# Layer norm roots of two tiles at once, gates ahead of the GLU, and GLU products in time order in a decoder trunk kernel

## The chip, the cores and the metric

The kernel runs on one core of one Trainium2 chip. Times are device microseconds of a whole execution. TensorE (PE) multiplies matrices, VectorE (DVE) and GpSimd (POOL) work on tensors elementwise, ScalarE (ACT) evaluates functions out of a table that has to be loaded, and SyncE (SP) issues most of the DMAs.

## The reference, cut to what matters

One layer of a hybrid recurrent trunk for a prompt of 2048 tokens and 32 sample tokens, with a model width of 1024. The part that the change touches, in short form:

```python
r  = sigmoid(xa_c @ w_r + b_r);  gi = sigmoid(xa_c @ w_i + b_i)   # RG-LRU gates, 8 heads of 64
log_a = -8 * r * softplus(-lam); a = exp(log_a)
mult = sqrt(-expm1(2 * log_a))
hseq = linear_scan(a, mult * gi * xa_c, h0)
y_a  = gelu(gate_a) * hseq
gy   = gelu(y_s)                                  # y_s: output of the S5 recurrence
y_b  = gy * sigmoid(gy @ glu_w + glu_b)           # the GLU
mix  = concat([y_a, y_b], -1) @ out_proj
x    = layer_norm(ALPHA * x + g1 * mix, ln1_g, ln1_b)
h    = x * (1 + sc2) + sh2                        # then the MLP, with a second layer norm
```

## The kernel before, in words

All matmuls keep single precision by splitting each operand into a high and a low part (`split`: ScalarE copies the high part, another engine subtracts to get the low part); a product is then three matmuls, high by high, high by low and low by high.

The program runs in stages. First come modulation, the input projection and the S5 recurrence. Then comes the stage of this change, from about 440 to 760 us: it walks over eight blocks `pi` of 256 tokens (the last has the 32 sample tokens too), and each block goes through

- `rg_gates`: eight PSUM tiles `pg` of three matmuls each; ScalarE takes a sigmoid of each into `rr` and `gi`, and a tanh of `rr` into `th`.
- `rg_scan`: ScalarE's exponential of `rr`, its square (into `xc`), VectorE's `th`, ScalarE's square root, GpSimd's products `gi`, VectorE's scan over time (`gi`), the product `gt`, and the split of `gt` into `yah` and `yal`.
- `glu_in` and `glu_block`: loads `gy` and splits it into `gyh` and `gyl`; four PSUM tiles `glu` of twelve matmuls each; a tanh on ScalarE (a sigmoid of half the argument), a product with `gy` on VectorE, and for every two of the four tiles a split into `ybh` and `ybl`. The S5 output lies in memory by (i, c), where a token's time is 8c+i; the split reads with a stride, so that `ybh` and `ybl` are in time order.
- `rg_conv`: the depthwise convolution that prepares the gates' operand `xc`, split into `xch` and `xcl`.
- `out_block`: for the two tiles of 128 tokens, two halves of 512 columns each, 24 matmuls of 512 columns into a PSUM tile `op`, VectorE's product with the gate row `g1r`, VectorE's sum with the residual `x`, then `norm`: statistics, the reciprocal root `rs` by an integer estimate and three Newton steps on columns of 128x1 (`rstd_of`), the normalization, eight transposes through PSUM tiles `nt`, and a store.

The loop works on several blocks at once: in pass `pi` it does the GLU of block pi+1, the gates of block pi+2, the out products of block pi, then the scan of block pi+2 and the convolution of block pi+3. A scheduler then orders each engine's instructions by readiness; the written order is its guide. Two things bind it: `after_all` lists that keep ScalarE's instructions of one table together (gates and GLU use tanh and sigmoid, the scan exponentials and square root), and the buffers. Gates and GLU take turns in the PSUM tags A and B, of two buffers each (`rot(GLU_BANKS)`), the out products in D and B (`rot(OUT_BANKS)`); so B is shared by all three. `raw_tile` gives the x tiles of `out_block` three buffers of 128x1024.

Of the kernel before, what the change touches and what calls it, by code (L numbers as in the profile page):

```python
# [9 lines left out]
F32 = mybir.dt.float32  # L10
# [3 lines left out]
ALU = mybir.AluOpType  # L14
# [12 lines left out]
L = 8  # L27
# [8 lines left out]
def trunk(ctx: ExitStack, tc: tile.TileContext, *args):  # L36
# [18 lines left out]
    def ts(eng, out, in0, s1, s2=None, op0=ALU.mult, op1=ALU.add):  # L55
        if s2 is None:
            eng.tensor_scalar(out, in0, s1, None, op0)  # L57
        else:
            eng.tensor_scalar(out, in0, s1, s2, op0, op1)

    def stt(out, in0, s, in1, op0=ALU.mult, op1=ALU.add):
        return V.scalar_tensor_tensor(out, in0, s, in1, op0, op1)  # L62
# [560 lines left out]
    ts(V, ab1, vec["ln1_b"], ALPHA, None, ALU.mult)  # L623
    add(V, AB, AB, ab1.unsqueeze(2).to_broadcast([P, KD, 9]))

    def rstd_of(pool, mv, nm, np_):
        r = pool.tile([P, 1], F32, tag="rstd", name=nm, bufs=2)[:np_]
        v = pool.tile([P, 1], F32, tag="rvar", name=nm + "v", bufs=2)[:np_]
        t = pool.tile([P, 1], F32, tag="rtmp", name=nm + "t", bufs=2)[:np_]
        ts(V, v, mv[:, 1:2], EPS, None, ALU.add)  # L630
        V.tensor_scalar(t.bitcast(I32), v.bitcast(I32), 1, None, ALU.arith_shift_right)
        V.tensor_scalar(r.bitcast(I32), t.bitcast(I32), -1.0, 1597463007.0, ALU.mult, ALU.add)
        ts(V, v, v, -0.5, None, ALU.mult)
        for _ in range(3):
# [204 lines left out]
    def glu_in(pi):  # L839
        last = pi == 7  # L840
        npr = 256
        n = npr + (TS if last else 0)
        c0, ncp = pi * 32, 32
        ncc = ncp + (16 if last else 0)
        if pi:
            gy = p4.tile([P, 4, 288], F32, tag="gy", name=f"gy{pi}")
        else:
            gy = raw_tile("gy0").rearrange("p (f t) -> p f t", f=4)
        for f in range(4):
            SP.dma_start(gy[:, f, :npr].rearrange("p (i c) -> p i c", i=L),  # L850
                         Yd[f, :, :, c0:c0 + ncp].rearrange("i p c -> p i c"))
        if last:
            Q.tensor_copy(gy[:, :, npr:n], ysm)
        if pi:
            gyh = p4.tile([P, 4, 288], F32R, tag="gyh", name=f"gyh{pi}")
            gyl = p4.tile([P, 4, 288], F32R, tag="gyl", name=f"gyl{pi}")
        else:
            gyh, gyl = (wslot("gy0", x, wpb).rearrange("p (f t) -> p f t", f=4) for x in "hl")
        split(gyh[:, :, :n], gyl[:, :, :n], gy[:, :, :n], Q)
        return gy, gyh, gyl  # L860

    gy0 = glu_in(0)
# [33 lines left out]
    def glu_block(pi):  # L896
        last = pi == 7
        npr = 256
        n = npr + (TS if last else 0)
        gy, gyh, gyl = glu_in(pi) if pi else gy0  # L900
        yh = p4.tile([P, 4, 288], F32R, tag="ybh", name=f"ybh{pi}", bufs=2)
        yl = p4.tile([P, 4, 288], F32R, tag="ybl", name=f"ybl{pi}", bufs=2)
        glu_t = []
        for m in range(4):
            ms = slice(m * P, m * P + P)
            ac = gate_ps[0](f"glu{pi}_{m}")
            for k in range(4):
                wh, wl = gw[k // 2]
                kk = k % 2
                PE.matmul(ac[:, :n], wh[:, kk, ms], gyh[:, k, :n], start=(k == 0), stop=False)  # L910
                PE.matmul(ac[:, :n], wh[:, kk, ms], gyl[:, k, :n], start=False, stop=False)
                PE.matmul(ac[:, :n], wl[:, kk, ms], gyh[:, k, :n], start=False, stop=(k == 3))
            glu_t.append(act(ac[:, :n], ac[:, :n], AF.Tanh, scale=0.5, bias=hgb[:, m:m + 1]))
            stt(gy[:, m, :n], ac[:, :n], 1.0, gy[:, m, :n], ALU.add, ALU.mult)
            if m % 2:
                ms = slice(m - 1, m + 1)
                split(yh[:, ms, 0:npr].rearrange("p f (c i) -> p f c i", i=L),
                      yl[:, ms, 0:npr].rearrange("p f (c i) -> p f c i", i=L),
                      gy[:, ms, 0:npr].rearrange("p f (i c) -> p f c i", i=L), V)
                if last:  # L920
                    split(yh[:, ms, npr:n].rearrange("p f (s j) -> p f s j", j=JS),
                          yl[:, ms, npr:n].rearrange("p f (s j) -> p f s j", j=JS),
                          gy[:, ms, npr:n].rearrange("p f (j s) -> p f s j", j=JS), Q)
        if pi:
            after_all(rgs[pi]["root"], glu_t)
        if pi < 7:
            rgs["glu", pi + 1] = glu_t
        return yh, yl

    def out_block(pi, ya, yb):  # L930
        t0 = pi * 256
        tiles = ([(256, TS, True)] if pi == 7 else []) + [(0, P, False), (P, P, False)]
        for ti, (o, w, smp) in enumerate(tiles):
            xt = raw_tile(f"x4_{pi}_{ti}")
            SP.dma_start(xt[:w, :], xs if smp else xp[t0 + o:t0 + o + w, :])
# [13 lines left out]
            for half in range(2):  # L949
# [26 lines left out]
    def norm(pi, ti, xt, w, smp, t, pool):

        st = pool.tile([P, 2, 6], F32, tag="st5", name=f"st_{pi}_{ti}", bufs=2)
        mv = pool.tile([P, 2], F32, tag="mv5", name=f"mv_{pi}_{ti}", bufs=2)
        for half in range(2):  # L980
            V.bn_stats(st[:w, half, :], xt[:w, half * 512:half * 512 + 512])
        V.bn_aggr(mv[:w], st[:w])
        rs = rstd_of(pool, mv[:w], f"rs4_{pi}_{ti}", w)
        ts(V, xt[:w], xt[:w], mv[:w, 0:1], rs, ALU.subtract, ALU.mult)
# [12 lines left out]
        (S if pi == 7 else SP).dma_start(Nd[:, :, t:t + w].rearrange("k p t -> p k t"), nT[:, :, :w])
# [901 lines left out]
```

## Time and profile before

| what | value |
|---|---|
| median of three runs | 2111.79 us (2110.53 to 2115.14) |
| the profiled execution | 2115.44 us, its span 2113.7 us |
| TensorE busy | 2011.9 us, 95% of the span |
| VectorE busy | 1543.5 us, 73% |
| ScalarE busy | 1087.4 us, 51% |
| GpSimd busy | 494.0 us, 23% |
| TensorE's mean granted clock | 0.986 of full |

The span is what the profiler saw of the program; the execution's time has 1.7 us more around it. The last chain of work, followed back from the end, is 63% TensorE and 19% VectorE. The shares are means over stages that differ: the stage of this change is the part from about 440 to 760 us, and behind it stands the MLP, where TensorE works almost without a pause.

### The profile page before, as it was taken

What the parts mean: (1) busy time and instruction counts of PE and PEld (TensorE: products, weight loads), DVE (VectorE), ACT (ScalarE), POOL (GpSimd) and SP (SyncE); (2) the same over time, 40 slices, a digit from 0 to 9 for tenths busy, and PEclk for the clock granted to TensorE, in tenths of its full rate; (3) what the DMA queues carried; (4) which work ended last, traced back from release to release, by engine and by line L of the source; (5) the groups of instructions that cost most, each with busy time, mean ns of one, the idle gap of its engine ahead of it and who ended that gap; (6) DMA issues with size and microseconds to landing.
All of it is one profiled execution on the core that took longest, in us unless ns stands there. A gap on an engine that the chain in (4) does not pass through costs nothing.

```text
span 2113.7 us, 35579 instructions
## 1 busy us (share of the span) xinstructions
PE 2011.9 (95%) x13055; PEld 1904.1 (90%) x13055; DVE 1543.5 (73%) x2920; ACT 1087.4 (51%) x2077; POOL 494.0 (23%) x327
## 2 busy tenths in 40 slices
PE   7998999889999989999999899999999999999996
PEld 4897888887877879999999899999999999999996
DVE  5678897467887899989898965666747555655587
ACT  3446665445766447554646454635445344444452
POOL 2255333323433233222223300101012001010103
PEclk9999999999999999999999999999999999999998
DMA  9799765543434467968677797878678968686861
GB/s 329 177 263 274 233 197 171 141 137 80 130 94 99 134 244 265 346 248 306 239 278 264 266 323 248 305 268 288 243 260 317 315 229 282 216 270 239 265 218 54
DMA packets 363037, 489.08 MB, mean 231 GB/s; under 512 B 126939, under 2 KB 264575, under 8 KB 362863
## 3 DMA queue, kind: packets, MB, share of 16 engines
q1 hardware_dynamic: 359415, 485.52, 69.6%
q8 instruction: 103, 1.69, 0.3%
q10 hardware_dynamic: 3448, 1.29, 0.2%
q14 instruction: 71, 0.58, 0.1%
HBM read 347.73 MB, written 139.00 MB: 230 GB/s over the span
## 4 chain that ended last, share of the span: by engine, by line
PE 63%; DVE 19%; DMA 6%; issue 5%; ACT 4%; POOL 1%; SPq 1%; ACTq 0%; DVEq 0%; POOLq 0%
PE m1a L1078 19%; PE m2x L1225 13%; PE m1s L1078 8%; PE m2s L1225 6%; PE m2a L1225 3%; DVE xc L62 2%; DVE acc L44 1%; PE accg L373 1%; PE accg L374 1%; PE accg L375 1%; PE op L963 1%; PE pa L185 1%; PE op L964 1%; PE op L962 1%; DVE gi L347 1%
## 5 line engine op out<-in xcount | busy, mean ns | idle before, releaser
L44 POOL TENSOR_TENSOR y<-y,ln_g 128x512 f32<-128x512 f32 (+3 forms) x28 | 36.5, 1320 | 645.8 <-ACT y L65 544.2
L65 ACT ACTIVATE hid<-hid 128x346 f32<-128x346 f32 (+1 forms) x240 | 116.1, 489 | 71.1 <-DVE hid L62 64.3
L65 ACT ACTIVATE ht<-hid 128x692 fp32r<-128x692 f32 (+1 forms) x92 | 72.0, 783 | 127.8 <-PE m2a L1225 38.9
L44 DVE TENSOR_TENSOR lt<-hid,ht 128x692 fp32r<-128x692 f32 (+1 forms) x92 | 85.2, 927 | 40.5 <-ACT ht L65 40.5
L44 DVE TENSOR_TENSOR acc<-m2x,acc 128x346 f32<-128x346 f32 (+1 forms) x168 | 84.1, 511 | 32.0 <-PE m2x L1225 31.7
L44 DVE TENSOR_TENSOR hid<-hid,hid 128x692 f32<-128x692 f32 (+1 forms) x92 | 87.1, 947 | 23.5 <-ACT hid L65 23.3
L1225 PE MATMUL m2x<-ht,hw2s 128*128 128x348 f32 (+1 forms) x352 | 87.7, 322 | 1.8 <-DVE acc L44 1.8
L62 DVE SCALAR_TENSOR_TENSOR hid<-m1s,vecB,u 128x346 f32<-128x346 f32 (+1 forms) x94 | 53.5, 573 | 45.0 <-ACT u L65 35.4
L65 ACT ACTIVATE u<-m1a 128x346 f32<-128x346 f32 (+1 forms) x96 | 43.5, 453 | 70.4 <-PE m1a L1078 63.0
L44 DVE TENSOR_TENSOR lb<-hid,hb 128x692 fp32r<-128x692 f32 (+1 forms) x69 | 69.2, 1004 | 4.7 <-ACT hb L65 4.5
L65 ACT ACTIVATE hb<-hid 128x692 fp32r<-128x692 f32 (+1 forms) x69 | 53.8, 783 | 21.6 <-PE m2a L1225 6.9
L1225 PEld LDWEIGHTS m2x<-ht,hw2s 128*128 128x128 f32 x352 | 61.9, 189 | 2.2 <-ACT hw2s L65 2.1
L65 ACT ACT_TABLE_LOAD x40 | 51.3, 1283 | 15.9 <-DVE hgb L57 6.5
L44 DVE TENSOR_TENSOR acc<-m2s,acc 128x346 f32<-128x346 f32 (+1 forms) x120 | 55.7, 508 | 4.1 <-PE m2s L1225 4.0
L1078 PE MATMUL m1s<-h2t13h,hw1s 128*128 128x348 f32 (+1 forms) x200 | 54.1, 329 | 3.9 <-DVE x L62 3.5
L1225 PE MATMUL m2x<-lt,hw2s 128*128 128x348 f32 (+1 forms) x176 | 56.1, 321 | 0.9 <-DVE lt L44 0.9
L1225 PE MATMUL m2x<-ht,w2s 128*128 128x346 f32 (+1 forms) x216 | 55.9, 321 | 0.0
L1225 PE MATMUL m2s<-ht,hw2s 128*128 128x348 f32 (+1 forms) x208 | 53.2, 331 | 2.6 <-ACT ht L65 2.6
L44 DVE TENSOR_TENSOR u<-m1s,u 128x346 f32<-128x346 f32 (+1 forms) x48 | 24.7, 514 | 42.0 <-PE m1s L1078 27.2
L65 ACT ACTIVATE y<-y,AB,mods 128x128 f32<-128x128 f32 (+2 forms) x96 | 37.5, 472 | 34.5 <-DMA y<-Cd 34.5
L1225 PE MATMUL m2a<-hb,hw2a 128*128 128x348 f32 (+1 forms) x200 | 52.0, 327 | 3.4 <-DVE acc L44 3.4
L1078 PE MATMUL m1a<-h2b1h,hw1a 128*128 128x348 f32 (+1 forms) x208 | 55.1, 323 | 0.0
(854 smaller groups left out, 7982.0 us busy)
## 6 DMA issues: line engine op xcount, KB each, us to landing
W1d<-hw1s SPq DMA_DIRECT2D x53, 512.0 KB
W2d<-hw2s SPq DMA_DIRECT2D x53, 512.0 KB
w1s<-W1d SPq DMA_DIRECT2D x45, 512.0 KB
lw1s<-W1d SPq DMA_DIRECT2D x43, 512.0 KB
hw2s<-W2d SPq DMA_DIRECT2D x41, 512.0 KB
hw1s<-W1d SPq DMA_DIRECT2D x40, 512.0 KB
w2s<-W2d SPq DMA_DIRECT2D x40, 512.0 KB
lw2s<-W2d SPq DMA_DIRECT2D x39, 512.0 KB
```

The source lines that it names most:

```text
L44: return eng.tensor_tensor(out=out, in0=in0, in1=in1, op=op)
L62: return V.scalar_tensor_tensor(out, in0, s, in1, op0, op1)
L65: return S.activation(out, in_, f, **kw).ins
L185: PE.matmul(pa[q:q + 32, :], cT[:, k + e, :], w[:, n * 512:n * 512 + 512], start=(k == 0), stop=(k == KD - 2), tile_position=(0, q))
L347: V.tensor_tensor_scan(gi[:, f, :n], rr[:, f, :n], gi[:, f, :n], 0.0 if pi == 0 else rgs["h"][:, f:f + 1], ALU.mult, ALU.add)
L373: PE.matmul(acc[:, :nt], wh[:, k, :], hh[:, kk, :nt], start=(k == 0), stop=False)
L374: PE.matmul(acc[:, :nt], wh[:, k, :], hl[:, kk, :nt], start=False, stop=False)
L375: PE.matmul(acc[:, :nt], wl[:, k, :], hh[:, kk, :nt], start=False, stop=(k == KD - 1))
L962: PE.matmul(ac[:w, :], yh[:, kk, o:o + w], wh[:, hs], start=(k == 0), stop=False)
L963: PE.matmul(ac[:w, :], yl[:, kk, o:o + w], wh[:, hs], start=False, stop=False)
L1078: PE.matmul(ps, x[:, k, :], h[:, k, o:o + w], start=(on is None and k + i == 0), stop=(k == 3 and i == 2), skip_group_check=on is not None)
L1225: PE.matmul(ps[2 * s_ + jj], x[:, f, js], h[:, f, :], start=(fresh and n + f + e == 0), stop=(n == len(pairs) - 1 and f + e == 3), skip_gr ...
```

## The change

Four edits in one stage. (1) The norm takes both tiles of a block together: two variances stand side by side in a 128x2 tile, and one root chain serves both; a Newton step is written as two products and one fused step where it was two fused steps. The last block's three tiles still go one by one. (2) The GLU product writes into a new tile `gp` in time order, and the split reads `gp` in a row; before, the product was written over `gy` and the split read with the stride. (3) The gates of block pi+2 are written ahead of the GLU of block pi+1, and the table order now puts the GLU's tanhs behind the first sigmoid of the next gates and ahead of the exponentials, in one table. (4) The low part `gyl` of the GLU's input is subtracted on VectorE, where GpSimd did it.

```diff
-    def rstd_of(pool, mv, nm, np_):
...
-        ts(V, v, mv[:, 1:2], EPS, None, ALU.add)
+    def rstd_of(pool, var, nm, np_):
+        r, v, t = (pool.tile([P, 2], F32, tag=tag, name=nm + tag, bufs=2)[:np_, :var.shape[1]]
+                   for tag in ("rstd", "rvar", "rtmp"))
+        ts(V, v, var, EPS, None, ALU.add)
...
         for _ in range(3):
-            stt(t, r, v, r, ALU.mult, ALU.mult)
+            mul(V, t, r, r)
+            mul(V, t, t, v)
             stt(r, t, 1.5, r, ALU.add, ALU.mult)
...
-        split(gyh[:, :, :n], gyl[:, :, :n], gy[:, :, :n], Q)
+        split(gyh[:, :, :n], gyl[:, :, :n], gy[:, :, :n], V)
...
+        gp = p4.tile([P, 4, 288], F32, tag="gp", name=f"gp{pi}")
...
-            stt(gy[:, m, :n], ac[:, :n], 1.0, gy[:, m, :n], ALU.add, ALU.mult)
+
+            stt(gp[:, m, 0:npr].rearrange("p (c i) -> p i c", i=L), ac[:, 0:npr].rearrange("p (i c) -> p i c", i=L), 1.0,
+                gy[:, m, 0:npr].rearrange("p (i c) -> p i c", i=L), ALU.add, ALU.mult)
+            if last:
+                stt(gp[:, m, npr:n], ac[:, npr:n], 1.0, gy[:, m, npr:n], ALU.add, ALU.mult)
             if m % 2:
                 ms = slice(m - 1, m + 1)
-                split(yh[:, ms, 0:npr].rearrange("p f (c i) -> p f c i", i=L),
-                      yl[:, ms, 0:npr].rearrange("p f (c i) -> p f c i", i=L),
-                      gy[:, ms, 0:npr].rearrange("p f (i c) -> p f c i", i=L), V)
+                split(yh[:, ms, 0:npr], yl[:, ms, 0:npr], gp[:, ms, 0:npr], V)
...
-        if pi:
+        if 0 < pi < 7:
+
+            after_all(rgs[pi + 1]["sig"][:1], glu_t)
+        elif pi:
             after_all(rgs[pi]["root"], glu_t)
         if pi < 7:
-            rgs["glu", pi + 1] = glu_t
+            rgs["glu", pi] = glu_t
...
+        if pi < 7:
+            norm(both_, p4)
...
+    def norm(tiles, pool):
+
+        pi, ti = tiles[0][:2]
+        w = tiles[0][3]
+        mv = pool.tile([P, 2, 2], F32, tag="mv5", name=f"mv_{pi}_{ti}", bufs=2)
+        for e, (_, ti_, xt, *_) in enumerate(tiles):
+            st = pool.tile([P, 2, 6], F32, tag="st5", name=f"st_{pi}_{ti_}", bufs=2)
+            for half in range(2):
+                V.bn_stats(st[:w, half, :], xt[:w, half * 512:half * 512 + 512])
+            V.bn_aggr(mv[:w, e, :], st[:w])
+        rs = rstd_of(pool, mv[:w, 0:len(tiles), 1], f"rs4_{pi}_{ti}", w)
+        for e, tile_ in enumerate(tiles):
+            norm_out(*tile_, mv[:, e, 0:1], rs[:, e:e + 1], pool)
...
     for pi in range(8):
+        if pi < 6:
+            rg_gates(rg, pi + 2)
         if pi < 7:
             ybs[pi + 1] = glu_block(pi + 1)
-        if pi < 6:
-            rg_gates(rg, pi + 2)
```

What the scheduler makes of it is seen in each engine's order. Names carry the block (glu3_1 is the second GLU tile of block 3) and a serial number. The first place is ScalarE around the GLU of block 3. Before, its tanhs have a table load on either side, and the gates of block 4 (rr4, gi4) come behind the second load:

```order
L65 ACTIVATE th3_6512<-th3_6512 128x4x256
L65 ACTIVATE yah3_6753<-gt3_6735 128x4x256
L65 ACT_TABLE_LOAD
L65 ACTIVATE glu3_0_6791<-glu3_0_6791,hgb_5928 128x256
L65 ACTIVATE glu3_1_6806<-glu3_1_6806,hgb_5928 128x256
L65 ACTIVATE glu3_2_6823<-glu3_2_6823,hgb_5928 128x256
L65 ACTIVATE ybh3_6789<-gy3_6780 128x2x256
L65 ACTIVATE glu3_3_6838<-glu3_3_6838,hgb_5928 128x256
L65 ACT_TABLE_LOAD
L65 ACTIVATE rr4_6855<-pg4_0_0_6858,vecB_250 128x256
```

Of the change, the same tanhs on ScalarE:

```order
L65 ACTIVATE rr4_6761<-pg4_3_0_6794,vecB_250 128x256
L65 ACTIVATE th4_6763<-rr4_6761,nla_100 128x256
L65 ACTIVATE gi4_6762<-pg4_2_1_6789,vecB_250 128x256
L65 ACTIVATE gi4_6762<-pg4_3_1_6799,vecB_250 128x256
L65 ACTIVATE glu3_0_6820<-glu3_0_6820,hgb_5928 128x256
L65 ACTIVATE xch5_7076<-xc5_7075 128x4x256
L65 ACTIVATE glu3_1_6835<-glu3_1_6835,hgb_5928 128x256
L65 ACTIVATE glu3_2_6852<-glu3_2_6852,hgb_5928 128x256
L65 ACTIVATE ybh3_6817<-gp3_6819 128x2x256
L65 ACTIVATE glu3_3_6867<-glu3_3_6867,hgb_5928 128x256
L65 ACT_TABLE_LOAD
L65 ACTIVATE rr4_6761<-rr4_6761,la_99 128x256 x4
```

The tanhs moved behind the gates of block 4 with no load between, the exponentials (rr4 out of la) follow one load later, and the conversion xch5 stands among the tanhs.

The second place is VectorE around a scan. Before, in block 3, the scan (gi3) and the product gt3 have steps of a root chain (rs4_1_0) around them:

```order
L631 TENSOR_SCALAR rs4_1_0t_6620<-rs4_1_0v_6619 128x1
L347 SCALAR_TENSOR_TENSOR gi3_6511<-rr3_6510,hp2_6405,gi3_6511 128x256 x4
L632 TENSOR_SCALAR rs4_1_0_6618<-rs4_1_0t_6620 128x1
L57 TENSOR_SCALAR rs4_1_0v_6619<-rs4_1_0v_6619 128x1
L350 COPY hp3_6750<-gi3_6511 128x4
L44 TENSOR_TENSOR gt3_6735<-gt3_6735,gi3_6511 128x4x256
L62 SCALAR_TENSOR_TENSOR rs4_1_0t_6620<-rs4_1_0_6618,rs4_1_0v_6619 128x1
L44 TENSOR_TENSOR op1_1_1_6675<-op1_1_1_6675,g1r_6052 128x512
L62 SCALAR_TENSOR_TENSOR rs4_1_0_6618<-rs4_1_0t_6620,rs4_1_0_6618 128x1
```

Of the change, VectorE around the scan of block 4:

```order
L62 SCALAR_TENSOR_TENSOR th4_6763<-xc4_6740,th4_6763 128x4x256
L44 TENSOR_TENSOR gyl4_7149<-gy4_7143,gyh4_7148 128x4x256
L44 TENSOR_TENSOR op2_0_1_6913<-op2_0_1_6913,g1r_6053 128x512
L347 SCALAR_TENSOR_TENSOR gi4_6762<-rr4_6761,hp3_6731,gi4_6762 128x256 x3
L44 TENSOR_TENSOR op2_1_0_6942<-op2_1_0_6942,g1r_6053 128x512
L347 SCALAR_TENSOR_TENSOR gi4_6762<-rr4_6761,hp3_6731,gi4_6762 128x256
L62 SCALAR_TENSOR_TENSOR x4_2_0_6884<-x4_2_0_6884,op2_0_1_6913 128x512
L62 SCALAR_TENSOR_TENSOR x4_2_1_6940<-x4_2_1_6940,op2_1_0_6942 128x512
L350 COPY hp4_7066<-gi4_6762 128x4
L44 TENSOR_TENSOR gt4_7051<-gt4_7051,gi4_6762 128x4x256
L995 BN_STATS st_2_0_6997<-x4_2_0_6884 128x6
```

The new subtraction gyl4 stands ahead of the scan, and behind the scan come the residual's sums and statistics where root steps stood.

The third place is TensorE where the gates begin. Before, the gates of block 3 (pg3) follow the GLU of block 2:

```order
L910 MATMUL glu2_3_6493<-gyh2_6440,hglu1_5924 128x256
L911 MATMUL glu2_3_6493<-gyl2_6441,hglu1_5924 128x256
L912 MATMUL glu2_3_6493<-gyh2_6440,lglu1_5925 128x256
L311 MATMUL pg3_0_0_6513<-xch3_6415,wgh_4961 128x256
L312 MATMUL pg3_0_0_6513<-xcl3_6416,wgh_4961 128x256
L313 MATMUL pg3_0_0_6513<-xch3_6415,wgl_4962 128x256
```

Of the change, the gates of block 4 on TensorE:

```order
L969 MATMUL op1_1_1_6634<-hwo7_5974,ybh1_6147 128x512
L970 MATMUL op1_1_1_6634<-hwo7_5974,ybl1_6148 128x512
L971 MATMUL op1_1_1_6634<-lwo7_5975,ybh1_6147 128x512
L311 MATMUL pg4_0_0_6764<-xch4_6741,wgh_4961 128x256
L312 MATMUL pg4_0_0_6764<-xcl4_6742,wgh_4961 128x256
L313 MATMUL pg4_0_0_6764<-xch4_6741,wgl_4962 128x256
L311 MATMUL pg4_1_0_6774<-xch4_6741,wgh_4961 128x256
L312 MATMUL pg4_1_0_6774<-xcl4_6742,wgh_4961 128x256
L313 MATMUL pg4_1_0_6774<-xch4_6741,wgl_4962 128x256
L969 MATMUL op2_0_0_6886<-hwo1_5938,yah2_6399 128x512
```

The gates now begin right behind the out products of block 1, with the out products of block 2 among them.

## Rows read from the trace of the kernel before

**Rows 1.** Windows: start:end, length, busy PE, PEld, DVE, ACT, POOL; clock, DMA share, GB/s

```profile
520.00:668.00 148.00, 135.16 (x741) 114.08 (x741) 126.18 (x288) 100.43 (x151) 56.51 (x27) 0.99 0.38 101
760.00:2113.00 1353.00, 1315.83 (x8240) 1304.28 (x8238) 970.12 (x1658) 663.75 (x1249) 231.69 (x157) 0.99 0.76 263
```

**Rows 2.** Timeline of TensorE, 505.9 to 518.7 us: start, duration, engine, line, operation

```profile
506.04 0.39 PE L963 MATMUL op<-hwo,ybl 128*128 128x512 f32 x1
...
514.19 0.28 PE L910 MATMUL glu<-gyh,hglu 128*128 128x256 f32 x1
...
518.31 0.28 PE L912 MATMUL glu<-gyh,lglu 128*128 128x256 f32 x1
```

**Rows 3.** Timeline of ScalarE, the first and last of six loads before exponentials

```profile
505.17 1.28 ACT L65 ACT_TABLE_LOAD   x1
...
681.26 1.28 ACT L65 ACT_TABLE_LOAD   x1
```

**Rows 4.** TensorE's waits, 466 to 668 us: who, for whom, total us, times, longest

```profile
PE pg L311 <- DVE gy L62: 4.4, 7, 1.2
PE glu L910 <- DVE x L62: 3.9, 3, 1.7
PE nt L995 <- DVE x L59: 3.6, 4, 2.4
PE op L962 <- ACT ybh L65: 2.9, 1, 2.9
PE op L963 <- DVE ybl L44: 1.2, 2, 0.9
```

**Rows 5.** Timeline of all engines, 520.9 to 525 us; brackets: idle before, releaser

```profile
521.01 0.15 DVE L62 SCALAR_TENSOR_TENSOR rs<-rs_0t,rs 128x1 f32<-128x1 f32 x1
...
521.59 2.37 POOL L44 TENSOR_TENSOR yal<-gt,yah 128x1024 fp32r<-128x1024 f32 x1 [5.27 <-ACT yah L65]
521.74 2.23 DVE L62 SCALAR_TENSOR_TENSOR rs_0t<-rs,rs_0v 128x1 f32<-128x1 f32 x1
...
523.90 0.41 DVE L62 SCALAR_TENSOR_TENSOR gy<-glu,gy 128x256 f32<-128x256 f32 x1
...
524.36 0.38 PE L311 MATMUL pg<-xch,wgh 128*128 128x256 f32 x1 [0.80 <-DVE gy L62]
```

**Rows 6.** Groups of VectorE by shape, 466 to 760 us: busy us, mean ns | idle

```profile
L44 DVE TENSOR_TENSOR ybl<-gy,ybh 128x512 fp32r<-128x512 f32 x16 | 18.5, 1156 | 2.0 <-ACT ybh L65 1.9
L62 DVE SCALAR_TENSOR_TENSOR rs_0t<-rs,rs_0v 128x1 f32<-128x1 f32 x21 | 13.7, 653 | 0.2
...
L62 DVE SCALAR_TENSOR_TENSOR gy<-glu,gy 128x256 f32<-128x256 f32 x28 | 11.5, 416 | 1.9 <-ACT glu L65 1.9
...
L44 DVE TENSOR_TENSOR gt<-gt,gi 128x1024 f32<-128x1024 f32 x5 | 6.1, 1218 | 0.0
...
L44 DVE TENSOR_TENSOR hw1a<-rw,hw1a 128x512 fp32r<-128x512 f32 x2 | 1.4, 677 | 2.7 <-ACT hw1a L65 2.7
```

**Rows 7.** Groups of ScalarE by shape, 466 to 760 us

```profile
L65 ACT ACT_TABLE_LOAD x28 | 35.9, 1283 | 7.4 <-DVE hgb L57 6.5 <-issue 0.4
L65 ACT ACTIVATE ybh<-gy 128x512 fp32r<-128x512 f32 x16 | 18.4, 1147 | 13.6 <-DVE gy L62 13.6
...
L65 ACT ACTIVATE hw1a<-rw 128x512 fp32r<-128x512 f32 x2 | 1.3, 626 | 5.1 <-DMA rw<-in_mlp_w_dram 5.1
```

**Rows 8.** Groups of GpSimd by shape, 466 to 760 us

```profile
L44 POOL TENSOR_TENSOR gyl<-gy,gyh 128x1024 fp32r<-128x1024 f32 x6 | 16.0, 2675 | 49.4 <-ACT gyh L65 49.4
```

**Rows 9.** The chain that ended last, 538 to 548 us: start, duration, what

```profile
540.28 5.05 DMA x<-in_x_prompt_dram
```

**Rows 10.** Timeline of ScalarE, 539 to 546 us

```profile
539.83 1.06 ACT L65 ACTIVATE xch<-xc 128x1024 fp32r<-128x1024 f32 x1 [1.40 <-DVE xc L62]
```

**Rows 11.** Windows of 20 us: columns as in rows 1

```profile
560.00:580.00 20.00, 20.00 (x98) 17.06 (x98) 13.08 (x32) 15.78 (x27) 7.34 (x4) 0.93 0.57 145
760.00:780.00 20.00, 17.08 (x90) 14.95 (x88) 18.84 (x42) 9.76 (x20) 7.10 (x4) 0.90 0.88 305
```

More of the change, by code (lines that the diff above doesn't have):

```diff
@@ L624, in trunk @@
     add(V, AB, AB, ab1.unsqueeze(2).to_broadcast([P, KD, 9]))
-    def rstd_of(pool, mv, nm, np_):
-        r = pool.tile([P, 1], F32, tag="rstd", name=nm, bufs=2)[:np_]
-        v = pool.tile([P, 1], F32, tag="rvar", name=nm + "v", bufs=2)[:np_]
-        t = pool.tile([P, 1], F32, tag="rtmp", name=nm + "t", bufs=2)[:np_]
-        ts(V, v, mv[:, 1:2], EPS, None, ALU.add)
+    def rstd_of(pool, var, nm, np_):
+        r, v, t = (pool.tile([P, 2], F32, tag=tag, name=nm + tag, bufs=2)[:np_, :var.shape[1]]
+                   for tag in ("rstd", "rvar", "rtmp"))
+        ts(V, v, var, EPS, None, ALU.add)
         V.tensor_scalar(t.bitcast(I32), v.bitcast(I32), 1, None, ALU.arith_shift_right)
@@ L922, in glu_block @@
                           yl[:, ms, npr:n].rearrange("p f (s j) -> p f s j", j=JS),
-                          gy[:, ms, npr:n].rearrange("p f (j s) -> p f s j", j=JS), Q)
-        if pi:
+                          gp[:, ms, npr:n].rearrange("p f (j s) -> p f s j", j=JS), Q)
+        if 0 < pi < 7:
+            after_all(rgs[pi + 1]["sig"][:1], glu_t)
+        elif pi:
             after_all(rgs[pi]["root"], glu_t)
         if pi < 7:
-            rgs["glu", pi + 1] = glu_t
+            rgs["glu", pi] = glu_t
         return yh, yl
@@ L932, in out_block @@
         tiles = ([(256, TS, True)] if pi == 7 else []) + [(0, P, False), (P, P, False)]
+        both_ = []
         for ti, (o, w, smp) in enumerate(tiles):
@@ L966, in out_block, with norm_out @@
                 stt(xt[:w, hs], xt[:w, hs], ALPHA, ac[:w, :])
-            work = lambda *x, at=(pi, ti, xt, w, smp, t0 + o): norm(*at, *x)
+            at = [(pi, ti, xt, w, smp, t0 + o)]
             if pi == 7 and ti in DEFER:
-                deferred.append(work)
-            else:
-                work(p4)
+                deferred.append(lambda pool, at=at: norm(at, pool))
+            elif pi == 7:
+                norm(at, p4)
+            else:
+                both_ += at
+        if pi < 7:
+            norm(both_, p4)
     DEFER = (1, 2)
     deferred = []
[L976 to L984, printed above, removed]
+    def norm(tiles, pool):
[10 more added lines that the diff above has]
+            norm_out(*tile_, mv[:, e, 0:1], rs[:, e:e + 1], pool)
+    def norm_out(pi, ti, xt, w, smp, t, mean, rs, pool):
+        ts(V, xt[:w], xt[:w], mean[:w], rs, ALU.subtract, ALU.mult)
         if smp:
```

## The prediction

> **What bounds the kernel now.** The profiled execution took 2115.4 us, a span of 2113.7 and 1.7 around it; the three runs shown have their median at 2111.8, so this execution lies 3.7 us above it. I make the sum against the 2115.4 and carry the difference over to the median unchanged.
>
> The view by windows comes first [rows 1]. The changed code runs before 760 us; in the 1353 us after it nothing is edited. So the change plays out in about 290 us, and its worth is what TensorE stands still there. In the steady blocks (520 to 668 us) TensorE is busy 135.2 us of 148, VectorE 126.2, ScalarE 100.4, GpSimd 56.5: TensorE ends last, with VectorE close behind it, at 85%.
>
> How long a block has to be comes from the spacing of matmuls at full clock [rows 2]: 35 steps with 512 columns from 506.04 to 514.19, 0.233 us each; 35 with 256 from 514.19 to 518.31, 0.118 each. A block of 256 tokens has 96 of the first and 72 of the second (24 for gates, 48 for GLU), 22.4 + 8.5 = 30.9 us, and 16 transposes besides. What a block takes is the distance of the exponentials' table loads: from 505.17 to 681.26 are five blocks [rows 3], 35.2 us each. Some 4 us a block are transposes and standstill.
>
> The view of TensorE's waits names the standstill [rows 4]. Gates wait for GLU products 7 times (4.4 us), GLU matmuls for residual adds (3.9), transposes for the normalized x (3.6), out products for the high and low parts of the GLU output (2.9 and 1.2). These five rows make 16.0 us in 202: the ceiling of what the order of work can bring.
>
> Why a product is late is seen in a timeline [rows 5]. A step of the root chain on a 128x1 column takes 0.15 us at 521.01; the same kind of step takes 2.23 at 521.74, and ends at 523.97 when GpSimd's subtraction yal (521.59 plus 2.37) ends. The GLU product starts behind it, at 523.90, and the gates' matmul at 524.36. VectorE's instructions with two tensors in SBUF stand still while GpSimd runs a tensor_tensor. [...]
>
> **The change, part by part.**
>
> *Order on TensorE (gates ahead of GLU).* The gates' first buffers, of tags A and B, were last read by the GLU's products long before and by the out block's adds; the GLU then follows the gates, whose readers are ScalarE's sigmoids. No gate comes right behind a product any more: T1, the 4.4 us of gates behind products, go: −4.4. Bounds 0 (another reader is as late) and −4.4. The 3.9 us for which GLU matmuls waited for the residual adds pass to the gates, which now take those banks first. They may stay whole (0) or go whole (−3.9), because the added 12 matmuls of work ahead give VectorE time; I take half, T2 = −2.0.
>
> *Norm of two tiles at once.* Root chains of 20 small instructions a pair become one of 13: seven fewer at 0.15 us [rows 5], −1.05 us of VectorE a block. More matters that 21 steps which wrote rs_0t took 653 ns in the mean [rows 6], so each can be caught behind GpSimd. Behind the scan now stand statistics and adds out of PSUM, one SBUF input each. On the other side the first tile's transposes come later, with the second's. T3, of the 3.6 us that transposes wait: a quarter, −0.9 (bounds 0 and −3.6). The last block does its three tiles alone, with 13 instructions where there were 10: nine more at 0.15 make T6 = +1.4, in a stretch (760 to 780 us) where VectorE is busy 18.8 us of 20 [rows 11]. Bounds 0 and +1.4.
>
> *GLU products in time order.* The product now writes with a stride of eight elements (32 bytes), and the split after it reads in a row. What the split gains stands in rows: the low part took 1156 ns [rows 6], a subtraction of the same size read in a row 677 (hw1a); the high part on ScalarE 1147 against 626 [rows 7]. Two halves a block: 0.96 us less on VectorE, 1.04 on ScalarE. What the strided write costs no row shows. Lower bound: nothing, the product stays at 416 ns [rows 6]. Upper bound: the same price for each element as the strided read, (1156−677)/2 = 0.24 us for 256 columns, four times 0.96 a block. I take the upper end, since the strided read is its nearest row; then VectorE gains nothing by this edit and ScalarE its 1.04. [...] The out products' wait for these parts: the last high and low parts come 0.52 and 0.48 us sooner after their product, and gates standing between cover up to 12×0.118 = 1.4. Of 4.1 us I let the first and a single piece of cover through: T4 = −1.9 (0 to −4.1).
>
> *One table for GLU and gates.* Three table loads a block instead of four; 40 become 36 in all, at 1.28 us [rows 7] 5.1 us of ScalarE. ScalarE has some 11 us a block free (47.6 of 148 us idle, of 35.2), so alone this is worth nothing; it shortens the way from yah to the gates. I cost it at nothing beyond T1 and T2. Its cover is that slack.
>
> *Conversions ahead of the GLU.* In some blocks xch, the split of the convolution, now stands among the GLU tanhs. It waited 1.40 us for VectorE's xc and took 1.06 in a block of before [rows 10]. Queued behind it are the tanhs, behind these the products, ybh, and the out products. Three blocks at 1.40 are 4.2 us on ScalarE; a third reaches TensorE, T7 = +1.4 (0 to +4.2).
>
> *gyl on VectorE.* GpSimd loses 2675 ns a block [rows 8]; VectorE gets it at the price of gt, the same shape with two inputs, 1218 ns [rows 6]. It cancels the −1.05 of the roots. It stands right before the scan, so the scan, gt and yah wait behind it; the out products read this yah only two blocks later, but on ScalarE the next gates' table load and sigmoids are queued behind yah, and TensorE's gates wait for their banks. Cost on the path: nothing while ScalarE's 11 free microseconds cover it; without cover 1.22 a block, 7.3 for six (rival A).
>
> [...]
>
> **Sum.** −4.4 −2.0 −0.9 −1.9 −1.4 +1.4 +1.4 = −7.8 us. Execution 2115.4 to 2107.6, median 2111.8 to 2104.0 (−0.37%). No change means within 0.2% (4.2 us), about what a measurement of this kernel can tell. With each term a third off, its own range is 2100 to 2108.
>
> **Rivals.**
>
> *A, same: the loop through ScalarE and VectorE sets the pace.* Gates, GLU tanh, exponential, square, root, scan, yah and the next gates now follow each other under fixed tables, on VectorE with gyl (1.22) and a product (0.66 with the upper bound) ahead of the scan. For it: VectorE is busy 85% of the stretch, so its queue has 5.2 us of a block's 35.2 left. Against it: two of three new pieces are paid for by the roots and the low parts. Then T1 and T2 come back as a wait for another reader, and −0.9 −1.9 +1.4 +1.4 leaves 0; 2109 to 2113. Chance 0.20.
>
> *B, slower: the pair keeps two of three raw buffers.* A tile's buffer was given back after its own transposes; now both come free after the pair's. The second x of the next block can be loaded only then. Such a load took 5.05 us and ended a chain that the residual add waited for [rows 9]. The add follows 11.2 us (48×0.233) after the first tile's; it decides when the transposes end less than 5.05 us ahead of the add. In VectorE's order, products and statistics stand behind it. At 3 us in six blocks, +18: −7.8 +18 is 2122. Against it: the pair's transposes stand ahead of half a block's matmuls. Chance 0.14.
>
> *C, more.* All five waits of [rows 4] go, 16.0, and the dip of 1.4, with T6 alone, +1.4, against them: −16.0, 2096. For it: every one has VectorE's queue at its root. Against: VectorE's load stays what it is. Chance 0.12.
>
> *D: the table does not merge.* The instructions as ordered have 36 loads, so this holds only if GLU tanhs come too late and stall it; 2112, chance 0.02.
>
> My forecast has 0.52. **Chances**: faster 0.50 + 0.12, and a hundredth of D, 0.63; same 0.02 + 0.20, 0.22; slower B and a hundredth, 0.15. **Range**: from C with T5 at −2.8 and T6 at 0, −18.8, 2093, to A's 2113 with T7 at its upper end, 2.8 more, 2116; it leaves B out.
>
> **What would show it.** Right: gates (pg) no longer wait for gy or gp; GLU waits for x gone or under 2 us; 36 table loads; exponentials' loads 33.5 to 34.5 us apart; products gp near 0.66 us, low parts near 0.68, gyl near 1.22; fewer root steps over 1 us. Wrong: x adds idle behind the DMA of x (B); scan or ybh behind gyl, with gates waiting for ScalarE (A); gp over 0.9 us; or a clock below 0.97 in a further stretch of 20 us.

## The result and the profile after

The change made the kernel slower: 2124.1 us median of six runs (2122.2 to 2127.3) against 2113.3 of before (2110.5 to 2115.1), a ratio of 1.0055 with a 95% interval of 1.0042 to 1.0068, so 9 to 14 us. The forecast was 2104, and its range ended at 2116. The profiled execution took 2127.05 us, 11.6 more than before's.

The waits of TensorE in the profile after, 466 to 668 us, answer to [rows 4]:

```profile
PE pg L311 <- DVE x L62: 7.5, 3, 5.4
PE nt L1013 <- DVE x L59: 5.9, 3, 3.4
PE pg L311 <- ACT rr L65: 2.4, 3, 1.1
PE pg L311 <- DVE gp L62: 1.9, 1, 1.9
PE op L969 <- DVE gp L62: 1.0, 1, 1.0
```

The gates wait for gy no more, but for x, rr and gp, 11.8 us in place of 4.4. The 3.9 us of GLU behind x, of which half was to go, are 7.5 of gates behind x; the transposes' wait for the normalized x went from 3.6 to 5.9. The sum is 18.7 us, against 16.0 for the five rows of before.

The windows of the profile after have the columns of [rows 1]:

```profile
520.00:668.00 148.00, 131.63 (x691) 109.54 (x690) 125.27 (x248) 84.28 (x136) 39.86 (x20) 0.97 0.36 98
```

VectorE issued 248 instructions where it had issued 288 and was busy as long, 125.3 us against 126.2. The two counts aren't for equal work: the pair norm takes away seven small steps a block, some thirty in this window, and TensorE got through fewer matmuls in it (691 against 741). What held the gates up is seen at their longest wait. The timelines of VectorE and GpSimd in the profile after, 645 to 661 us:

```profile
651.50 2.39 POOL L44 TENSOR_TENSOR gi<-gi,th 128x1024 f32<-128x1024 f32 x1 [2.75 <-ACT th L65]
...
652.33 2.63 DVE L44 TENSOR_TENSOR gyl<-gy,gyh 128x1024 fp32r<-128x1024 f32 x1 [2.44 <-ACT gyh L65]
654.89 0.68 DVE L44 TENSOR_TENSOR op<-op,g1r 128x512 f32<-128x512 f32 x1
655.49 2.66 DVE L347 TENSOR_TENSOR_SCAN gi<-rr,hp,gi 128x256 f32<-128x256 f32 x4
658.08 0.66 DVE L62 SCALAR_TENSOR_TENSOR x<-x,op 128x512 f32<-128x512 f32 x1
```

and that of TensorE, 652 to 660 us:

```profile
653.02 0.40 PE L969 MATMUL op<-hwo,yah 128*128 128x512 f32 x1
658.79 0.61 PE L311 MATMUL pg<-xch,wgh 128*128 128x288 f32 x1 [5.37 <-DVE x L62]
```

VectorE waits 2.44 us for ScalarE's gyh, then gyl takes 2.63 us (1.22 was its price): GpSimd's product has been running when gyl starts, and gyl ends 1.07 us after that product, which ended at 653.89. Then come the scans, and the residual sum that gives the gates their buffer starts at 658.08. TensorE stands for 5.4 us.

### The profile page after: what moved, and what is told of

Its sections match the earlier page's. It is cut to its first block, busy times and chain, and to the rows that moved or that the text cites. A ratio compares the mean times of both kernels' runs of the same rounds, so it can differ in the third digit from the quotient of the medians.

```text
span 2125.3 us, 35513 instructions
## 1 busy us (share of the span) xinstructions
PE 2018.1 (95%) x13055; PEld 1908.6 (90%) x13055; DVE 1546.3 (73%) x2892; ACT 1074.1 (51%) x2073; POOL 484.9 (23%) x319
## 4 chain that ended last, share of the span: by engine, by line
PE 63%; DVE 19%; DMA 6%; issue 4%; ACT 4%; POOL 2%; SPq 1%; ACTq 0%; DVEq 0%; POOLq 0%
PE m1a L1096 19%; PE m2x L1243 13%; PE m1s L1096 8%; PE m2s L1243 6%; PE m2a L1243 3%; DVE xc L62 2%; DVE acc L44 1%; PE pa L185 1%; DMA xa<-Xd 1%; PE accg L373 1%; PE accg L374 1%; DVE hw2s L44 1%; PE accg L375 1%; PE op L970 1%; PE op L971 1%
## 5 line engine op out<-in xcount | busy, mean ns | idle before, releaser
L44 DVE TENSOR_TENSOR lb<-hid,hb 128x692 fp32r<-128x692 f32 (+1 forms) x69 | 63.7, 925 | 6.2 <-ACT hb L65 6.1
L969 PE MATMUL op<-hwo,yah 128*128 128x512 f32 x128 | 52.0, 407 | 3.2 <-ACT os L65 2.2
L62 DVE SCALAR_TENSOR_TENSOR E<-E,et 128x16 f32<-128x16 f32 (+3 forms) x128 | 46.1, 399 | 10.3 <-ACT et L65 10.1
```

What stands on the lines that cost most here:

```text
L44: return eng.tensor_tensor(out=out, in0=in0, in1=in1, op=op)
L969: PE.matmul(ac[:w, :], yh[:, kk, o:o + w], wh[:, hs], start=(k == 0), stop=False)
```

## The experiments

Each kernel was timed beside the kernel before; the ratio is to that, with its 95% interval. The parts are called norm (both tiles at once), gyl (on VectorE), product (GLU products in time order) and order (gates ahead, one table).

| kernel | median us | ratio | interval |
|---|---|---|---|
| the change | 2124.1 | 1.0055 | 1.0042 to 1.0068 |
| without gyl (m1) | 2125.2 | 1.0064 | 1.0050 to 1.0078 |
| without order (m2) | 2111.4 | 0.9997 | 0.9988 to 1.0006 |
| without norm (m3) | 2116.2 | 1.0016 | 1.0005 to 1.0028 |
| without product (m4) | 2118.3 | 1.0026 | 1.0016 to 1.0037 |
| order alone (o1) | 2129.9 | 1.0081 | 1.0067 to 1.0095 |
| norm alone (o2) | 2117.1 | 1.0026 | 1.0016 to 1.0035 |
| without order, last block's steps fused (o3) | 2110.9 | 0.9992 | 0.9983 to 1.0001 |
| change, out products in own buffers (o4) | 2125.6 | 1.0059 | 1.0045 to 1.0072 |
| change, two rr and gi (x1) | 2124.9 | 1.0061 | 1.0048 to 1.0074 |
| without order, one table (x2) | 2112.7 | 1.0002 | 0.9992 to 1.0013 |
| gyl and product alone (x3) | 2111.0 | 0.9999 | 0.9987 to 1.0011 |
| the same, one table (x4) | 2116.3 | 1.0019 | 1.0009 to 1.0030 |
| without gyl, two rr and gi (y1) | 2122.5 | 1.0049 | 1.0037 to 1.0061 |
| change, two rr and gi, own buffers (y2) | 2128.6 | 1.0079 | 1.0067 to 1.0091 |
| the same without gyl (y3) | 2127.1 | 1.0071 | 1.0059 to 1.0083 |
| without order, two rr and gi (y4) | 2111.7 | 0.9997 | 0.9986 to 1.0008 |
| change, less GpSimd work (h1) | 2115.2 | 1.0014 | 1.0002 to 1.0026 |
| without order, less GpSimd work (h2) | 2112.2 | 1.0009 | 0.9999 to 1.0019 |

**Which part.** In m1 gyl goes back to GpSimd:

```diff
-        split(gyh[:, :, :n], gyl[:, :, :n], gy[:, :, :n], V)
+        split(gyh[:, :, :n], gyl[:, :, :n], gy[:, :, :n], Q)
```

> All of the change except that gyl stays on GpSimd. The change is 10.9 us slower than before (2124.1 against 2113.25). Theory 1 (gyl on VectorE stands in the queue ahead of the residual adds, waits there for ScalarE's gyh and for GpSimd, and the gates wait for the adds): most of the 5 to 6 us that the stage loses by 760 us comes back, so 2115 to 2119, and gates wait for x under 3 us instead of 7.5. Theory 2 (the gates' place ahead of the GLU, in buffers shared with the adds): 2122 to 2126, no change. Theory 3 (the pair norm): 2122 to 2126. Theory 4 (a small shift that the MLP stage answers with other clock pieces): scattered, 2116 to 2126, with the loss behind 760 us differing between kernels.

In m2 the loop and the table lists are those of before:

```diff
-        if pi < 6:
-            rg_gates(rg, pi + 2)
         if pi < 7:
             ybs[pi + 1] = glu_block(pi + 1)
+        if pi < 6:
+            rg_gates(rg, pi + 2)
```

> All of the change except the order: GLU ahead of the gates and the table lists as before. Theory 1 (gyl in VectorE's queue): 2120 to 2126. Theory 2 (gates need buffers that the residual adds read last): back to 2110 to 2116. Theory 3 (pair norm): 2120 to 2126. Theory 4: scattered, by the part behind 760 us.

In m3 norm and rstd_of are those of before, called for each tile:

```diff
-                both_ += at
-        if pi < 7:
-            norm(both_, p4)
+                work(p4)
```

> All of the change except the pair norm: each tile has its own root chain and its own transposes as before. Theory 3 (both tiles' transposes late, raw buffers given back late): 2112 to 2117, and the wait of transposes for x falls from 5.9 to under 3 us. Theories 1 and 2: 2120 to 2126. Theory 4: scattered, by the part behind 760 us.

In m4 the product goes over gy again:

```diff
-            stt(gp[:, m, 0:npr].rearrange("p (c i) -> p i c", i=L), ...
+            stt(gy[:, m, :n], ac[:, :n], 1.0, gy[:, m, :n], ALU.add, ALU.mult)
```

> All of the change except the GLU products in time order: the product goes over gy and the split reads with the stride. If the edit is worth what its durations say (low and high parts shorter, the product longer), this is 0 to 6 us slower than the change, 2124 to 2130. If the strided write cost more on VectorE than the split gains, it is faster, 2118 to 2123. Theory 4: scattered, by the part behind 760 us.

Without the order the loss is gone: 1.0055 to 0.9997, some 12 us. With gyl back on GpSimd nothing is gained, and the gates still wait 6.9 us for x, so theory 1, which the timeline above suggests, falls as it was put. But m1 trades one hold for another: in four blocks the four scans, 2.7 us together, take 4.7 to 4.8 behind GpSimd's gyl. Norm and product are worth 8 and 6 us when left out (m3 and m4 came within what theory 3 and the strided write had forecast, 2112 to 2117 and 2118 to 2123), but only beside the order, as the next kernels show. o1 is the kernel before with the edit of the order alone; o2 is the kernel before with the norm alone.

> The kernel before with only the order changed (gates ahead of the GLU, and the table lists). Undoing the order brought 12.7 us (2124.1 to 2111.4), undoing another part at most 8. Theory 2 (the order is the loss by itself): 2120 to 2126, and gates wait for x and for ScalarE's rr. Rival (the order costs only together with the pair norm and the new tile, whose removal brought 7.9 and 5.8): 2111 to 2117.

> The kernel before with only the pair norm. Theory 2: within 3 us of before, 2110 to 2116. Theory 3 (the pair norm holds the adds back whatever the order is): 2117 to 2123. If its worth in the steady blocks is that of the sum (about -2) and its price is in the last block, the stage gains 1 to 4 us by 690 us and loses them between 690 and 830.

The order alone costs 0.81%, 17 us, more than the whole change and more than theory 2 allowed (2126). The norm alone costs 0.26%, which theory 2 did not expect (2110 to 2116), though it is free beside gyl and product (m2 against x3, 0.9997 and 0.9999). The parts don't add up. In o2 the wait of rival B stands in VectorE's waits, 500 to 700 us:

```profile
DVE x L62 <- DMA x<-in_x_prompt_dram: 8.3, 2, 4.2
```

In the change itself that row has 0.6 us: rival B isn't what happened there.

x3 has gyl and product alone; x2 and x4 take one table without moving the gates, by a sigmoid of one column; o3 is m2 with the fused steps of before for single tiles.

```diff
+        first = act(one, hgb[:, 0:1], AF.Sigmoid)
...
+            after_all(rgs[pi]["root"], [first])
+        after_all([first], glu_t)
```

> The kernel before with gyl on VectorE and the GLU products in time order, nothing else. The pair norm alone cost 5.2 us; with these two parts beside it the time is level with before. If the parts add up: 2105 to 2108. If the pair norm costs only where VectorE is busy with the old steps, and pays here: 2110 to 2114.

> The kernel with the old order (2111.4), but a sigmoid of a single column ahead of the GLU's tanhs, so that tanhs and the next gates' sigmoids stand under one table with no load between, 36 loads in all. If a table load in the loop costs its 1.28 us in each block: 6 to 9 us less, 2102 to 2106. If ScalarE's slack hides the load: 2109 to 2113.

> As the one before, with the single-column sigmoid that merges the tables. If parts add up and the load counts: 2098 to 2104. If the loads are hidden: as the one before.

```diff
+            if var.shape[1] == 1:
+                stt(t, r, v, r, ALU.mult, ALU.mult)
```

> As the kernel with the old order, but a root chain of a single tile (the last block's three) takes fused steps as before, 10 instructions instead of 13. The old order's kernel leads before by some 8 us in TensorE's work near 690 us and has given back 6.5 of them by 830. If the nine small instructions in a stretch where VectorE is full cause that: 2105 to 2109. If something else bounds the change of stages (clock pieces behind a standstill, or the arrival of data): 2109 to 2113, no difference.

x3 is level with before, so gyl and product bring nothing; x2 is level with m2, so a table load saved in each block is worth nothing. In x4 it even costs 4 us against x3, which neither forecast had and which stays open. o3 doesn't differ from m2: the nine small instructions don't show.

**Why the order costs.** Three things that could make the gates wait were taken away, alone and together.

```diff
-    GLU_BANKS, OUT_BANKS = "AB", "DB"
+    GLU_BANKS, OUT_BANKS = "AB", "D"
...
-        rr = rg_tile(rg, f"rr{pi}", "rr")
-        gi = rg_tile(rg, f"gi{pi}", "gi")
+        rr = rg_tile(rg, f"rr{pi}", "rr", bufs=2)
+        gi = rg_tile(rg, f"gi{pi}", "gi", bufs=2)
```

The first edit is o4, the second x1; y1 is the second with gyl on GpSimd, y2 both edits, y3 both with gyl on GpSimd, y4 the second on m2.

> The changed kernel, with the out products in PSUM tag D alone, so that gates and GLU share no buffer with the residual adds. Theory 2a (the price of the order is the shared buffers): the 7.5 us in which gates wait for x go, 2112 to 2118. Theory 2b (VectorE's queue is late whatever the buffers are): out products wait for the adds in their place, 2122 to 2130.

> The changed kernel with two buffers each for rr and gi in place of one. Theory 5 (with the order changed, a closed loop sets the pace: exponential, root, scan, then the next sigmoids, which overwrite the rr that the scan reads, then the GLU's tanhs, then the next exponential; 37.1 us a block against 35.2 before): the sigmoids no longer wait for the scan (5.4 to 6 us in places), exponentials come 33 to 35.5 us apart, and the time is 2108 to 2117. Rival (VectorE's queue with the adds is the pace, the loop only follows): exponentials stay 36.5 to 37.5 us apart, 2121 to 2127.

> The change with gyl on GpSimd and two buffers each for rr and gi. One at a time neither helped: without gyl gates waited for ScalarE's rr (7.2 us) in place of x, with two rr for x (10.5 us) in place of rr. Theory 6 (the two limits, the loop through rr and VectorE's queue, lie next to each other, so only lifting both gains): 2112 to 2118. Rival (the order leaves TensorE no other work while the adds are late, whatever they wait for): 2121 to 2127, with the wait for x still over 5 us.

> The change with two rr and gi and the out products in tag D alone. Theory 6: 2114 to 2120, since gates wait neither for x nor for rr, and gyl still stands ahead of the adds. Rival: out products wait for x in place of the gates, 2121 to 2127.

> The change with all three: gyl on GpSimd, two rr and gi, out products in tag D alone. Theory 6: 2110 to 2116. Rival: 2120 to 2126.

> The kernel with the old order (2111.4) and two buffers each for rr and gi: a control, and a candidate. If the loop through rr paces the old order too: 2104 to 2109. If not: 2109 to 2114.

None of the five brings it back: 2122.5 to 2128.6, and y2 and y3 lie even above the 2127 and 2126 of their rivals. In x1 the exponentials' table loads stay 37.0 us apart (37.1 in the change, 35.2 before), as its rival had it. y4, the control, is level with m2. The waits only change their name. TensorE's longest rows, 466 to 668 us, in o4, then x1, then y3:

```profile
PE op L969 <- DVE x L62: 9.7, 4, 3.0
PE pg L311 <- ACT rr L65: 5.6, 2, 3.2
```

```profile
PE pg L311 <- DVE x L62: 10.5, 5, 4.9
PE pg L311 <- DVE gp L62: 7.3, 1, 7.3
```

```profile
PE nt L1013 <- DVE x L59: 9.9, 3, 4.1
PE pg L311 <- ACT rr L65: 7.0, 2, 4.2
```

With buffers of their own the out products wait for x in the gates' place; with two rr the gates wait for x and gp in rr's place; with all three it is the transposes, and the gates again for rr. Whatever TensorE comes to next, VectorE or the work behind it is late. So I looked at VectorE over the same part of its work: from the first scan of block 2 to that of block 7. The windows, with the columns of [rows 1], are of before, of the change, and of m2:

```profile
516.40:692.40 176.00, 163.16 (x880) 138.00 (x879) 144.28 (x327) 119.50 (x179) 64.81 (x31) 0.98 0.38 100
```

```profile
504.00:691.50 187.50, 170.23 (x925) 143.64 (x924) 151.95 (x299) 107.35 (x174) 50.99 (x26) 0.97 0.36 94
```

```profile
512.90:682.00 169.10, 162.49 (x897) 138.13 (x897) 135.76 (x296) 112.99 (x178) 50.92 (x27) 0.99 0.38 104
```

The change and m2 issue almost the same VectorE work (299 and 296 instructions), but it takes 152.0 us in the one and 135.8 in the other. Idle time is alike, 35.5 and 33.3. Of the 18.4 us between the spans 16.2 are longer instructions. Not all of the 18.4 are lost: TensorE has 28 more matmuls in the change's stretch, and at the end of the stage, read below, the change is 9.3 us behind. The groups of VectorE by shape, 466 to 760 us, name them; first the change, then m2:

```profile
L44 DVE TENSOR_TENSOR ybl<-gp,ybh 128x512 fp32r<-128x512 f32 x16 | 14.2, 885 | 13.9 <-ACT ybh L65 13.9
L44 DVE TENSOR_TENSOR gyl<-gy,gyh 128x1024 fp32r<-128x1024 f32 x6 | 11.5, 1924 | 6.6 <-ACT gyh L65 6.6
L57 DVE TENSOR_SCALAR rs_0rvar<-mv 128x2 f32<-128x2 f32 x7 | 5.6, 807 | 0.2
L44 DVE TENSOR_TENSOR rs_0rtmp<-rs_0rstd 128x2 f32<-128x2 f32 x21 | 5.6, 265 | 0.4
```

```profile
L44 DVE TENSOR_TENSOR ybl<-gp,ybh 128x512 fp32r<-128x512 f32 x16 | 12.5, 784 | 0.9 <-ACT ybh L65 0.7
L44 DVE TENSOR_TENSOR gyl<-gy,gyh 128x1024 fp32r<-128x1024 f32 x6 | 8.9, 1485 | 4.0 <-ACT gyh L65 4.0
L44 DVE TENSOR_TENSOR rs_0rtmp<-rs_0rstd 128x2 f32<-128x2 f32 x21 | 3.4, 161 | 0.3
L57 DVE TENSOR_SCALAR rs_0rvar<-mv 128x2 f32<-128x2 f32 x7 | 1.3, 187 | 0.2
```

The same instructions take longer in the new order. If that is GpSimd's doing, the price must go with GpSimd's work. h1 is the change and h2 is m2, both with this edit for blocks 2 to 7:

```diff
-        mul(Q, gi[:, :, :n], gi[:, :, :n], xc[:, :, :n])
...
-        split(yh[:, :, :n], yl[:, :, :n], gt[:, :, :n], Q)
+            act(yh[:, :, :n], gt[:, :, :n], AF.Copy)
+            Q.memset(f32(yl[:, :, :n]), 0.0)
```

and the same for xch and xcl, so the low parts are zeros and one product is left out.

> The change, with three of GpSimd's four tensor_tensors of a block left out from block 2 on: the low parts xcl and yal are filled with zeros by a write that reads no tensor, and the product of gi and xc is left out. Theory 7 (in the new order more of VectorE's two-tensor instructions fall on GpSimd's, and stand still: by their durations above the shortest of their kind 31 us between the scans of blocks 2 and 7, against 19 in the old order, while VectorE's idle time is equal): the hold falls under 15 us, and the time from 2124 to 2108 to 2115. Rival (TensorE lacks other work in the new order, whatever VectorE does): 2119 to 2125.

> The same cut in the kernel with the old order (2111.4). Theory 7: the hold falls from 19 to under 12 us and the time by less than that of the new order's kernel, to 2104 to 2109, so that the two orders differ by under 6 us in place of 12.7. Rival: the two orders still differ by 10 to 15.

The new order's kernel came from 1.0055 to 1.0014, the old order's didn't move beyond its interval (0.9997 and 1.0009). The two orders, 12 us apart, are 1 us apart by the ratios and 3 by the medians. h1's 2115.2 lies just above the upper end of theory 7 (2115) and below the rival's 2119. The windows from scan to scan, of h1 and then h2:

```profile
503.70:682.70 179.00, 167.23 (x925) 142.44 (x924) 135.71 (x299) 106.95 (x174) 24.80 (x21) 0.99 0.36 99
```

```profile
508.70:679.10 170.40, 160.63 (x883) 136.28 (x883) 129.35 (x295) 113.48 (x179) 25.53 (x22) 0.99 0.38 103
```

In h1 the 299 instructions of VectorE take 135.7 us, as in m2. That the old order gained nothing, where 2104 to 2109 was expected, is a miss of theory 7 and says that its kernel doesn't hang on this.

Less GpSimd work could also help by sooner results. In the change, 504 to 691.5 us, VectorE alone waits for them, 3.2 us in all:

```profile
DVE gi L347 <- POOL gi L44: 1.6, 2, 1.2
DVE gi L44 <- POOL gi L44: 1.6, 1, 1.6
```

The second row stays as it is in h1, so at most 1.6 of the 8.5 us by which h1's stretch is shorter are such waits.

The kernel before belongs beside these, and it shows that more holding isn't what the order does. Its stretch has 144.3 us of VectorE; m2 has 8.5 less and is no faster. I counted, from scan to scan, the VectorE instructions that took over 0.25 us more than the shortest of their operation and shape while a GpSimd tensor_tensor ran, and added up the excess: 19 us in before (15 instructions), 8 in m2 (6), none in h2; 20 in the change (13), 5 in h1 (4). (Counted as in the forecasts, with GpSimd at rest too, the 31 and 19 fell to 16 and 13, not quite under 15 and 12, and before has 34.) In the old order 19, 8 and 0 us go with ratios of 1, 0.9997 and 1.0009; in the new one 20 and 5 go with 1.0055 and 1.0014. I read this as: the old order hides such holds from TensorE and the new one doesn't. The sum isn't a price there either: m3 has 20 us (14 instructions) and 1.0016. Which of the holds TensorE pays for isn't shown.

How much of the loss lies in the stage is read from TensorE's first product for the sample tile (oq), with as many matmuls behind it in each kernel. The timelines of TensorE, of before, the change, m2, h1 and h2 in turn:

```profile
735.32 0.64 PE L946 MATMUL oq<-hwo,ysum 128*32 128x256 f32 x8 [0.58 <-DVE ysum L44]
```

```profile
741.10 1.08 PE L953 MATMUL oq<-hwo,ysum 128*32 128x256 f32 x8 [0.38 <-DVE ysum L44]
```

```profile
731.83 1.08 PE L950 MATMUL oq<-hwo,ysum 128*32 128x256 f32 x8 [0.38 <-DVE ysum L44]
```

```profile
733.17 1.08 PE L962 MATMUL oq<-hwo,ysum 128*32 128x256 f32 x8 [0.39 <-DVE ysum L44]
```

```profile
735.04 1.08 PE L959 MATMUL oq<-hwo,ysum 128*32 128x256 f32 x8 [0.51 <-DVE ysum L44]
```

The change is there 5.8 us behind before and 9.3 behind m2, and with less GpSimd work the new order is no later than the old (h1 1.9 us ahead of h2). Behind this point the change needs 1384.2 us (2125.3 − 741.1), m2 1378.9, before 1378.4, h1 1382.7. So of the 11.6 us between the two profiled executions only half lies in the stage. The other half is of the MLP, where no code differs. TensorE's longest wait for acc there is 2.9 us in the change and 1.8 before, and in the 259 us behind the point the granted clock is 0.98 against 0.99; but h2 has a wait of 2.9 too and needs 1375.6. Over the seventeen kernels with as many matmuls behind the point (to within six), one execution each, this part takes from 1372 us to the change's 1384, and in o1, the slowest kernel, 1376; so it doesn't go with the order. It stays open.

## Why the prediction was wrong

*The step that failed is T1 with T2*, the order on TensorE: −6.4 forecast, and some +12 measured by leaving it out, +17 by itself. Of T1's 4.4 us for products 1.9 stayed, and 7.5 for x and 2.4 for rr came. The wait's root was not the place behind a product: VectorE was late, and the next buffer's reader stood in the same queue. T2 took half of the wait for x as gone, and its bounds let it stay whole at the most; it almost doubled, 3.9 to 7.5. The sum had no term for VectorE standing behind GpSimd in the new order, although [rows 5] show that price: 2.08 us for a step of 0.15. Taking GpSimd's work out (h1) brought back three quarters of the loss, 0.41 of 0.55%; in the old order the same cut brought nothing. The new order isn't held more than the kernel before, 20 us against 19; what failed is the belief that it hides such delays from TensorE better. Why the gates' place exposes them, and the half of the loss behind the stage, isn't settled.

*The reading of the bound was too simple ahead of it.* I took TensorE as what ends last in the stage, from busy shares, and did not read the chain of waits there. The chain of before, 500 to 680 us, grouped by line:

```profile
by line: DVE xc L62 11.2%; issue 7.5%; DVE gi L347 7.0%; DVE rs_0t L62 6.0%; DVE ybl L44 5.1%; DVE st L981 4.4%; DVE th L62 4.3%; DVE x L62 3.7%; DMA gt<-Gd 3.6%; DMA gy<-Yd 3.4%; DMA x<-in_x_prompt_dram 2.8%; DVE gy L62 2.7%; DVE op L44 2.
```

VectorE's lines lead it, and none of those shown is a matmul's. VectorE isn't the bound throughout either, since m2 saves 8.5 us of it and no time. Windows of before, with the columns of [rows 1], show the two engines taking turns:

```profile
620.00:640.00 20.00, 17.21 (x96) 14.46 (x95) 19.93 (x57) 10.94 (x19) 3.50 (x4) 1.00 0.29 83
640.00:660.00 20.00, 20.00 (x111) 17.17 (x110) 15.42 (x28) 14.03 (x17) 10.46 (x4) 1.00 0.45 108
```

VectorE is full in the first and TensorE in the second. The mean shares, 85% and 91%, hide this.

*The rest came out in its sum only.* Norm, gyl and product together were T3, T4 and T6, −0.9 −1.9 +1.4 = −1.4; m2 measured 0.9997, −0.6 us with an interval of −2.5 to +1.3, so no effect at all fits as well. The parts were not confirmed: the norm alone cost 0.26% (o2) where T3 and T6 make +0.5 us, and beside the order norm and product cost 8 and 6 us. That the sum fits is in part luck. Their durations came as forecast where nothing held them: the product takes 657 ns (0.66 was the upper end that I took), the high part 627 (626), gyl 1.22 in h2. That the loads are hidden by ScalarE's slack was right too (36 loads, x2 level). T5, −1.4 for the clock, had the wrong sign: with more standstill the granted clock was 0.97 in 520 to 668 us where it had been 0.99. No run shows the −1.4 by itself (0.07 of the 20 us at 0.93 in [rows 11], the dip of rival C too): in the change 560 to 580 us has 0.92, and from scan to scan m2 has 0.99 where before has 0.98. T6 doesn't show (o3). T7 wasn't measured by itself.

*The rivals.* A named the loop through ScalarE and VectorE, and in the change ScalarE does wait up to 6 us for a scan before a gates' table; but with two rr (x1) the time stayed, so the loop through rr is not the limit by itself, and its price of 2109 to 2113 was too low. B had the sign and 2122, near the measured 2124.1, by a mechanism that the change doesn't show; that nearness is luck.

## What to carry to other kernels

Where two engines hold each other up, the order of instructions is a cost of its own: add up, over equal work, how long the same instructions take in both orders, and see who else is busy at the time. Count the kernel before too, and take the suspected work out in both orders: here as much holding cost nothing in the one and some 9 us in the other. Read the chain of waits and short windows of the stage before naming its bound from mean busy shares; two engines at 85% and 91% can take turns. And when a wait goes from a list of waits, ask which late engine stood behind it: as long as it is as late, lifting one wait only renames it, as buffers, a second rr and gyl did here.

## What the runs showed of the hardware

The prediction says that VectorE's instructions with two tensors in SBUF stand still while GpSimd runs a tensor_tensor. In before, 500 to 700 us, 19 of them began beside one, and 17 ended with it or later. The other two, steps of the convolution at 535.96 and 605.92, took 0.49 and 0.48 us as elsewhere, and GpSimd's products beside them 3.16 and 2.84 where 2.4 is common.

An instruction of VectorE with a single tensor as input was held too. The timeline of the change, 621.5 to 626 us:

```profile
622.94 2.39 POOL L44 TENSOR_TENSOR yal<-gt,yah 128x1024 fp32r<-128x1024 f32 x1 [6.58 <-ACT yah L65]
623.20 2.16 DVE L57 TENSOR_SCALAR rs_0rvar<-mv 128x2 f32<-128x2 f32 x1
625.40 0.17 DVE L630 TENSOR_SCALAR rs_0rtmp<-rs_0rvar 128x2 int32<-128x2 int32 x1
```

The step on 128x2 ends when GpSimd's ends, 2.16 us in place of 0.17; four of the seven steps of this kind took 0.7 us or more. Before, on 128x1 (one on 32x1), none of the seventeen took over 0.16, and eight of them ran beside a GpSimd tensor_tensor. A normalization of 128x1024 with one tensor was held too, once in the change: 2.83 us at 559.80 in place of 0.8, beside GpSimd's xcl (559.73 to 562.09). Why the step on 128x2 was held and those on 128x1 were not isn't shown. So the wider root chain, shorter by seven instructions, gained a step that was held four times.
